# A four-stage decoder step: loading the SGU's output weights two tiles early, building two tables by doubling, and turning a constant later

## The chip, the cores and the metric

One NeuronCore of a Trainium2 chip runs the whole program. TensorE does the matrix products and transposes (through PSUM), VectorE, ScalarE and GpSimd the elementwise work, and SyncE issues nearly all DMAs. The metric is the device time of one execution in microseconds (us), the median of several runs. Lower is better.

## What is computed

One inference step of a decoder with two layers over 1024 prompt tokens and 8 sample tokens, all in float32. Layer 0 mixes tokens with a spatial gating unit (SGU), layer 1 with a sparse attention over the keys that an indexer picks. A gated convolutional MLP (ConvGLU) follows each. Every sub-layer is modulated by scales, shifts and gates from `c`, and is closed by a LayerNorm. Cut to what the change touches:

```python
def sgu_mixer(h, w_in, b_in, norm_g, norm_b, w_s, b_s, w_out):
    z = jax.nn.gelu(h @ w_in + b_in)
    u, v = jnp.split(z, 2, axis=-1)
    v = layer_norm(v, norm_g, norm_b)
    ...
    return (u * mixed) @ w_out, v          # w_out: 1024 x 1024, the "output pieces"

xp = post_norm(xp, yp, mp[:, 2], ln_g[i, 0], ln_b[i, 0])     # LayerNorm(ALPHA*x + (1+gate)*y)
fp, cp = conv_glu(modulate(xp, ...), ...)                    # a, u = h @ w_up; (gelu(conv(a)) * u) @ w_down

s_idx = sum over heads of relu(qi . ki) * wi                 # the indexer's scores
_, sel = lax.top_k(s_idx, n_keep)                            # 256 of 1024 keys, or 128 of 513 for a sample
```

## The kernel before

**Data and products.** The activations lie transposed, features on partitions and 1032 tokens along the free dimension, in three chunks `CH` of 384, 384 and 264 tokens. A float32 product is made of three fast ones: the weights are split into a high and a low half (`whi`, `wlo`), the activations too (`Hh`, `Hl`), and `mm3` (lines 86 to 89) adds hi x hi, hi x lo and lo x hi. `dense` (line 156) makes one 128-column weight piece times one chunk: 8 x 3 = 24 matmuls into a PSUM bank `psA`.

**Weights.** `load_w` (line 108) loads a piece of 512 KB with one DMA on SyncE into a `raw` buffer (three in all, shared with the loads of `ada_round` and some scratch), and `split` (line 99) makes the two halves. Its `eng` names the two engines: "GG" is GpSimd for both, "AV" ScalarE for the high and VectorE for the low half. The halves lie by default in the pool W (four buffers, so two pieces), or, if `pool` is given, in one of the tags T (13 buffers), P (2) and E (2).

**The order of instructions.** The text of the program is the order of priority. A planner that lays out the instructions when the program is built puts on each engine what is ready earliest by its own estimates, hands out the buffers of a tag in the order of the program, and sets the waits; on the chip each engine then runs its own list strictly in order.

**The end of the SGU.** The loop at line 605 makes the eight U tiles with pieces 8 to 15, while `pump` hands out steps from a queue `fq`: from i = 12 on the eight loads and products of `ada_round(0, 2)` and its end, in which VectorE adds at line 258. With the last piece (i = 15) the product of U and V is split into `Hh` (ScalarE) and `Hl` (VectorE, line 106), chunk by chunk. At the end of every turn `zload(i + 2)` (line 320) loads one piece: pieces 14 and 15 are the last of the input weights, and 16 to 23 are the eight output pieces, called 0 to 7 below (`dt` in the code). Pieces 0 and 1 go to W, the others to T; 2 to 7 are loaded behind the loop, at line 626.

**The output projection** (`out_proj`, line 640) runs over the three chunks and, in each, over the eight output pieces, so a piece is used three times and given back after its use in chunk 2. VectorE accumulates each result into R (`accumulate`, line 634). Behind a chunk `ln_steps` (line 406) is put into `fq`: `t1` normalises three blocks of 128 tokens (transposes into two `psB` banks, of four; statistics on VectorE, three small operations on GpSimd, two writes by ScalarE, line 400, into a tile `n`), and `t2` turns them back, eight times, and applies scale and shift (`apply`, line 365: ScalarE lines 371 and 379, VectorE 372, GpSimd's `Hl` 377). The first block's `n` of a chunk is an E tile, the second's a P tile, the third's a raw buffer. The first ConvGLU tile then takes E for `As` and P for `Cc` (line 699), and `wload` its weights.

**Constants of the sparse attention** (lines 795 to 831) are made between the ConvGLU of layer 0 and the indexer's projections: `bits` and `pows`, 31 powers of two as integers and as floats, one column at a time; `rmask`, a mask of 128 x 8, and its transpose `ET`, by one transpose on TensorE and one copy on VectorE. `bits` and `pows` are read by the searches for the k-th largest score (`search`, line 935), `ET` by the samples' attention (line 1321). `sample_scores` (line 1040) is the queue's part that scores the samples' keys.

Of the kernel before, what the change touches and what calls it, by code (L numbers as in the profile page):

```python
# [13 lines left out]
OP = mybir.AluOpType  # L14
# [6 lines left out]
T = NPT + NB  # L21
# [34 lines left out]
def hybrid_step(  # L56
# [7 lines left out]
    V, A, G, PE, SP = nc.vector, nc.scalar, nc.gpsimd, nc.tensor, nc.sync  # L64
# [12 lines left out]
    def Tt(name, dt=F32, tag="T", n=SLOT):  # L77
        return tp.tile([128, n], dt, name=name, tag=tag, bufs=BUFS[tag])

    def bank(tag="A"):  # L80
        return psum.tile([128, 512], F32, name="ps" + tag, tag="ps" + tag)
# [17 lines left out]
    def split(hi, lo, src, e_hi, e_lo):  # L99
        if e_hi == "A":  # L100
            A.activation(hi, src, AF.Copy)  # L101
        elif e_hi == "G":
            G.tensor_scalar(hi, src, 1.0, 0.0, op0=OP.mult, op1=OP.add)  # L103
        else:
            V.tensor_copy(hi, src)
        (V if e_lo == "V" else G).tensor_tensor(lo, src, f(hi), op=OP.subtract)  # L106

    def load_w(src, cols, pool=None, eng="GG"):

        n = KT * cols  # L110
        raw = raws.tile([128, SLOT], F32, name="raw", tag="raw")
        SP.dma_start(raw[:, :n].rearrange("p (k c) -> p k c", k=KT), src.rearrange("(k p) c -> p k c", p=128))
        if pool:
            hi, lo = Tt("whi", F32R, pool), Tt("wlo", F32R, pool)
        else:
            hi = wp.tile([128, SLOT], F32R, name="whi", tag="W")
            lo = wp.tile([128, SLOT], F32R, name="wlo", tag="W")
        split(hi[:, :n], lo[:, :n], raw[:, :n], eng[0], eng[1])
        return (hi[:, :n].rearrange("p (k c) -> p k c", k=KT), lo[:, :n].rearrange("p (k c) -> p k c", k=KT))
# [25 lines left out]
    fq = deque()  # L145

    def pump(n=1):
        for _ in range(n):
            if fq:
                fq.popleft()()  # L150

    def drain():
        while fq:
            fq.popleft()()

    def dense(w, cols, c, tag="A"):
        c0, n = CH[c]
        b = bank(tag)
        for k in range(KT):
            mm3(b[:cols, :n], (w[0][:, k, :cols], w[1][:, k, :cols]), (Hh[:, k, c0:c0 + n], Hl[:, k, c0:c0 + n]),  # L160
                k == 0, k == KT - 1)
        return b
# [21 lines left out]
    def tr(out, in_):  # L184
        PE.transpose(out, in_, ident[:in_.shape[0], :in_.shape[0]])  # L185
# [7 lines left out]
    b = bank("B")  # L193
# [124 lines left out]
    pieces = {}  # L318

    def zload(i):  # L320
        if i < 16:
            m = zorder[i]
            pieces[i] = load_w(win[:, m * 128:(m + 1) * 128], 128, eng="AV" if i < 2 else "GG")
        elif i < 24:
            dt = i - 16
            pieces[i] = load_w(sgu_w_out[0][:, dt * 128:(dt + 1) * 128], 128, pool=[None, None, "T", "T", "T", "T", "T", "T"][dt])


    def mod(L, i):
# [104 lines left out]
    b = bank("B")  # L434
# [103 lines left out]
    b = bank("B")  # L538
# [62 lines left out]
    def product(m, c):  # L601
        c0, n = CH[c]
        V.tensor_tensor(VT[m][:, c0:c0 + n], VT[m][:, c0:c0 + n], U[m][:, c0:c0 + n], op=OP.mult)

    for i in range(8, 16):
        m = i - 8
        U[m] = Tt("U", tag="PPTT"[m % 4])
        for c in range(3):
            b = dense(pieces[i], 128, c)
            c0, n = CH[c]  # L610
            A.activation(U[m][:, c0:c0 + n], b[:, :n], AF.Gelu_apprx_tanh, bias=PAR[:, pSBI + m:pSBI + 1 + m])
            pump(2 if i < 12 else 1)
            if i > 11:
                product(m, c)
            if i == 15:
                for k in range(8):
                    split(Hh[:, k, c0:c0 + n], Hl[:, k, c0:c0 + n], VT[k][:, c0:c0 + n], "A", "V")
        if i == 11:
            drain()
            for c in range(3):  # L620
                for k in range(4):
                    product(k, c)
            fq.extend(ada_round(0, 2, rawmk))
        zload(i + 2)
    drain()
    for i in range(18, 24):
        zload(i)
    gate = gates(0, 2, "g02")

# [168 lines left out]
    def carve(n, p=128):  # L798
        v = misc[:p, at[0]:at[0] + n]
        at[0] += n  # L800
        return v

    cmin, m01, bits, pows = carve(128), carve(256), carve(31).bitcast(I32), carve(31)
    onec, rmask, rep, ET, PN = carve(1), carve(8), carve(128, 8), carve(128, 8), carve(128, 8)
# [6 lines left out]
    V.memset(m01[:, 0:128], 0.0)  # L811
    V.tensor_scalar(m01[:, 128:256], cmin, 0.0, NEG, op0=OP.is_lt, op1=OP.mult)
    V.memset(onec, 1.0)
    for i in range(31):
        V.memset(bits[:, i:i + 1], 1 << i)
        V.memset(pows[:, i:i + 1], 0.5 * (1 << i))
    V.memset(rmask, 1.0)
    rv = rmask.rearrange("p (j e) -> p j e", e=2)
    G.affine_select(out=rv, in_=rv, pattern=[[-32, 4], [-8, 2]], compare_op=OP.is_ge, fill=0.0, base=0, channel_multiplier=1)
# [4 lines left out]
    for e in range(2):  # L824
        G.affine_select(out=rr[:, :, e, :], in_=rr[:, :, e, :], pattern=[[0, 4], [1, 8]], compare_op=OP.is_equal, fill=0.0, base=0,
                        channel_multiplier=-1)
    b = bank("B")
    tr(b[:8, 0:128], rmask)
    V.tensor_copy(ET, b[:8, 0:128])
    junk = Tt("junk", BF, n=2 * SLOT)  # L830
    junkV, junkA = junk[:, 0:1024], junk[:, 1024:2048]

# [207 lines left out]
    def sample_scores():  # L1040

        kc = [Tt("kc"), Tt("kc")]
        st = {}

        def load(h):
            for s in range(4 * h, 4 * h + 4):
                gather(kc[h][:, (s % 4) * 256:(s % 4 + 1) * 256], cki, s)

        def pair(ss):
            if not st:  # L1050
                st["p"] = bank("A")
            kt = Tt("kt", tag="E")
            for i, s in enumerate(ss):
                b = bank("B")
                for r in range(4):
                    o = (s % 4) * 256 + r * 64
                    tr(b[0:64, r * 128:(r + 1) * 128], kc[s // 4][:, o:o + 64])
                A.activation(kt[0:64, i * 512:(i + 1) * 512].rearrange("d (p r) -> d r p", r=4),
                             b[0:64, :].rearrange("d (r p) -> d r p", r=4), AF.Copy)
            for i, s in enumerate(ss):  # L1060
                r0, e = 32 * (s // 2), s % 2
                PE.matmul(st["p"][r0:r0 + 32, :512], QSI[:, s, :], kt[0:64, i * 512:(i + 1) * 512], start=(e == 0), stop=(e == 1),
                          skip_group_check=True)
        def end():
            SS = Spk[3][0][:, 512:1026]
            rl = rawmk()
            A.activation(rl[:, :512], st["p"], AF.Relu, scale=0.125)
            pn = bank("B")
            for s in range(NB):
                r0, e = 32 * (s // 2), s % 2  # L1070
                PE.matmul(pn[r0:r0 + 32, :8], QSI[:, s, :], kiT, start=(e == 0), stop=(e == 1), skip_group_check=True)
            A.activation(rl[:, 512:520], pn[:, :8], AF.Relu, scale=0.125)
            b = bank("B")
            mm(b[:, :8], rep, wisT, True, True)
            V.tensor_tensor(WM, b[:, :8], rmask, op=OP.mult)
            b, b2 = bank("B"), bank("B")
            mm(b[:8, :512], WM, rl[:, :512], True, True)
            mm(b2[:8, :8], WM, rl[:, 512:520], True, True)
            V.tensor_copy(SS[:8, :512], b[:8, :512])
            V.tensor_tensor(t88, b2[:8, :8], ident[0:8, 0:8], op=OP.mult)  # L1080
            V.tensor_reduce(SS[:8, 512:513], t88, axis=AX.X, op=OP.add)
            V.memset(SS[:8, 513:514], 0.0)
            starts("s")

        return [lambda: load(0), lambda: load(1)] + [lambda x=x: pair(x) for x in ((0, 2), (1, 3), (4, 6), (5, 7))] + [end]
# [4 lines left out]
    def starts(key):  # L1090
        ready.add(key)
        for name, eng, keys in PLAN:
            if key in keys and ready.issuperset(keys):
                items = [(k, S(k), 128, 128 * (k + 1), KEEP_P) if k != "s" else (k, Spk[3][0][:8, 512:512 + NS], 8, NS, KEEP_S)
                         for k in keys]
                sq[eng].append(search(name, items, eng))
# [3 lines left out]
    for c in range(3):  # L1100
        while c not in spilled:
            pump()
        ki_part(c)
        pump(PUMP[c])
        for t in range(4):
            qi_part(t, c)
            if (t, c) == (0, 2):
                dload(5)
                dload(6)
            pump(PUMP[c])  # L1110
            spin(*SPIN[0])
        fq.append(lambda c=c: ki_rows(c))
        for b in blocks_of(c):
            if 2 <= b < 8:
                fq.extend(idx_steps(b))
                fq.append(lambda b=b: starts(b))
    fq.extend(sample_scores())


# [31 lines left out]
    for w in range(2):  # L1151
        kf = [Tt("kf0", tag="P"), Tt("kf1", tag="P")]
        for kvh in range(2):
            i = 5 + 2 * w + kvh
# [3 lines left out]
            for c in range(3):  # L1158
                b = dense(pcs[i], 128, c)
                c0, n = CH[c]  # L1160
# [334 lines left out]
```

## Time and profile before

| | us |
|---|---|
| median of 3 runs (lowest to highest) | 2628.93 (2626.52 to 2629.45) |
| the profiled execution | 2626.55 |
| its span, first to last instruction | 2624.8 |
| TensorE busy in it | 2525.8 (96%) |
| VectorE / GpSimd / ScalarE busy | 1676.1 / 998.4 / 793.2 |
| its mean granted TensorE clock | 0.981 of full |

The span starts at 0, and all times below are from there. The SGU's input products run to about 290 us, its output projection to about 398, the first ConvGLU to about 1215, the sparse attention to about 1800 and the second ConvGLU to the end. A row of a timeline gives the start, the duration, the engine, the line, the operation, what it writes and reads and the count; in brackets stands how long the engine was idle before it, and what it waited for last by the profile. Such a releaser is inferred: where the engine named had long been done, it was another, often a DMA. Operations of one engine can overlap in the rows, since they are pipelined.

### The profile page before, as it was taken

What the parts mean: (1) busy time and instruction counts of PE and PEld (TensorE: products, weight loads), DVE (VectorE), ACT (ScalarE), POOL (GpSimd) and SP (SyncE); (2) the same over time, 40 slices, a digit from 0 to 9 for tenths busy, and PEclk for the clock granted to TensorE, in tenths of its full rate; (3) what the DMA queues carried; (4) which work ended last, traced back from release to release, by engine and by line L of the source; (5) the groups of instructions that cost most, each with busy time, mean ns of one, the idle gap of its engine ahead of it and who ended that gap; (6) DMA issues with size and microseconds to landing.
All of it is one profiled execution on the core that took longest, in us unless ns stands there. A gap on an engine that the chain in (4) does not pass through costs nothing.

```text
span 2624.8 us, 41121 instructions
## 1 busy us (share of the span) xinstructions
PE 2525.8 (96%) x15984; PEld 2369.4 (90%) x15984; DVE 1676.1 (64%) x3913; ACT 793.2 (30%) x1611; POOL 998.4 (38%) x1066
## 2 busy tenths in 40 slices
PE   7999999999999999999999989998999999999996
PEld 5898898999999999998887979777999999999996
DVE  4233346677677767755798987534767677767647
ACT  3121234111111111124576776542311111111121
POOL 3332535233222322335346665534523333222335
PEclk8999999999999999999999989999999999999998
DMA  8314302222222222111114112233211111111111
GB/s 274 124 51 127 105 17 71 91 81 73 89 81 81 89 66 96 60 34 51 60 39 118 42 47 65 69 121 109 65 49 49 49 49 41 41 49 49 49 41 67
DMA packets 203977, 192.15 MB, mean 73 GB/s; under 512 B 9806, under 2 KB 178246, under 8 KB 202999
## 3 DMA queue, kind: packets, MB, share of 16 engines
q1 hardware_dynamic: 200582, 179.86, 21.8%
q0 software_dynamic: 2688, 9.44, 1.1%
q8 instruction: 127, 2.08, 0.3%
q14 instruction: 67, 0.55, 0.1%
q10 hardware_dynamic: 513, 0.23, 0.0%
HBM read 178.41 MB, written 11.27 MB: 72 GB/s over the span
## 4 chain that ended last, share of the span: by engine, by line
PE 80%; DVE 11%; POOL 3%; issue 2%; ACT 2%; DMA 2%; ACTq 0%; SPq 0%; POOLq 0%; DVEq 0%
PE psA L84 50%; PE psB L84 23%; PE psB L185 3%; PE psB L245 2%; DVE Cc L714 2%; DVE junk L948 1%; DVE R L634 1%; PE psA L185 1%; ACT junk L979 1%; DVE S L928 1%; POOL L L1252 0%; DMA raw<-in_dsa_w_out_dram 0%; DMA adaw<-in_w_ada_dram 0%; DVE R L638 0%; PE psA L1308 0%
## 5 line engine op out<-in xcount | busy, mean ns | idle before, releaser
L84 PE MATMUL psA<-Hh,whi 128*128 128x384 f32 (+1 forms) x2896 | 935.6, 324 | 14.7 <-POOL whi L103 7.7
L84 PE MATMUL psA<-Hl,whi 128*128 128x384 f32 (+1 forms) x2896 | 932.4, 322 | 0.1
L84 PE MATMUL psA<-Hh,wlo 128*128 128x384 f32 (+1 forms) x2896 | 929.1, 321 | 0.9 <-DVE wlo L106 0.9
L634 DVE SCALAR_TENSOR_TENSOR R<-psB,g,R 128x384 f32<-128x384 f32 (+1 forms) x952 | 525.6, 568 | 296.0 <-PE psB L84 293.8
L103 POOL TENSOR_SCALAR whi<-raw 128x1024 fp32r<-128x1024 f32 x179 | 194.8, 1089 | 1100.7 <-PE psA L84 962.2
L84 PEld LDWEIGHTS psA<-Hh,whi 128*128 128x128 f32 x2896 | 548.0, 189 | 44.8 <-issue 21.5
L84 PEld LDWEIGHTS psA<-Hl,whi 128*128 128x128 f32 x2896 | 548.6, 189 | 7.2 <-issue 6.1
L84 PEld LDWEIGHTS psA<-Hh,wlo 128*128 128x128 f32 x2896 | 547.9, 189 | 7.6 <-issue 5.0
L106 POOL TENSOR_TENSOR wlo<-raw,whi 128x1024 fp32r<-128x1024 f32 x163 | 403.6, 2476 | 12.7
L84 PE MATMUL psB<-gh,whi 128*128 128x384 f32 (+1 forms) x1056 | 341.9, 324 | 3.4 <-DVE t L637 1.6
L84 PE MATMUL psB<-gl,whi 128*128 128x384 f32 (+1 forms) x1056 | 337.7, 320 | 0.0
L84 PE MATMUL psB<-gh,wlo 128*128 128x384 f32 (+1 forms) x1056 | 337.7, 320 | 0.0
L714 DVE SCALAR_TENSOR_TENSOR Cc<-As,PAR,Cc 128x256 f32<-128x256 f32 (+3 forms) x264 | 262.2, 993 | 56.1 <-ACT Cc L709 54.9
L84 PEld LDWEIGHTS psB<-gh,whi 128*128 128x128 f32 x1056 | 198.4, 188 | 25.6 <-issue 13.8
L84 PEld LDWEIGHTS psB<-gl,whi 128*128 128x128 f32 x1056 | 198.6, 188 | 0.0
L84 PEld LDWEIGHTS psB<-gh,wlo 128*128 128x128 f32 x1056 | 198.5, 188 | 0.0
L101 ACT ACTIVATE gh<-Cc 128x384 fp32r<-128x384 f32 x132 | 64.9, 492 | 437.7 <-DVE Cc L721 437.6
L716 ACT ACTIVATE Cc<-Cc 128x384 f32<-128x384 f32 x132 | 64.9, 492 | 391.2 <-DVE Cc L714 391.2
L708 ACT ACTIVATE As<-psA 128x384 f32<-128x384 f32 x132 | 60.5, 458 | 341.5 <-PE psA L84 341.5
L721 DVE TENSOR_TENSOR Cc<-psA,Cc 128x384 f32<-128x384 f32 x132 | 67.8, 513 | 111.9 <-PE psA L84 111.3
L84 PE MATMUL psB<-Hh,wh 128*128 128x384 f32 (+1 forms) x512 | 137.8, 339 | 1.0 <-POOL wh L103 0.5
L638 DVE TENSOR_TENSOR R<-R,t 128x8 f32<-128x8 f32 x328 | 131.0, 406 | 2.9
(362 smaller groups left out, 3299.6 us busy)
## 6 DMA issues: line engine op xcount, KB each, us to landing
raw<-in_ffn_w_up_dram SPq DMA_DIRECT2D x88, 512.0 KB
raw<-in_w_ada_dram SPq DMA_DIRECT2D x64, 512.0 KB
raw<-in_ffn_w_down_dram SPq DMA_DIRECT2D x44, 512.0 KB
adaw<-in_w_ada_dram SPq DMA_DIRECT2D x32, 512.0 KB
raw<-in_sgu_w_in_dram SPq DMA_DIRECT2D x16, 512.0 KB
raw<-in_dsa_w_in_dram SPq DMA_DIRECT2D x16, 512.0 KB
raw<-in_dsa_w_out_dram SPq DMA_DIRECT2D x32, 256.0 KB
raw<-in_sgu_w_out_dram SPq DMA_DIRECT2D x8, 512.0 KB
```

What stands on the lines that cost most here:

```text
L84: PE.matmul(out, l, r, start=start, stop=stop)
L101: A.activation(hi, src, AF.Copy)
L103: G.tensor_scalar(hi, src, 1.0, 0.0, op0=OP.mult, op1=OP.add)
L106: (V if e_lo == "V" else G).tensor_tensor(lo, src, f(hi), op=OP.subtract)
L185: PE.transpose(out, in_, ident[:in_.shape[0], :in_.shape[0]])
L245: PE.matmul(st["b"][32 * g:32 * g + 32, :512], SCT[:, k, :], rw[g // 2][:, (g % 2) * 512:(g % 2 + 1) * 512], start=(k == 0), stop=(k == KT ...
L634: V.scalar_tensor_tensor(R[c][:, dt, :npr], b[:, :npr], gp[:, dt:dt + 1], R[c][:, dt, :npr], op0=OP.mult, op1=OP.add)
L638: V.tensor_tensor(R[c][:, dt, npr:n], R[c][:, dt, npr:n], t8, op=OP.add)
L708: A.activation(As[:, c0:c0 + n], b[:, :n], AF.Copy)
L714: V.scalar_tensor_tensor(Cc[:, a0:c0 + npr], As[:, a0 - d:c0 + npr - d], w, Cc[:, a0:c0 + npr], op0=OP.mult, op1=OP.add)
L716: A.activation(Cc[:, c0:c0 + n], Cc[:, c0:c0 + n], AF.Gelu_apprx_tanh)
L721: V.tensor_tensor(Cc[:, c0:c0 + n], b[:, :n], Cc[:, c0:c0 + n], op=OP.mult)
```

## The change

The load of the output pieces is moved up and spread. At the end of the turn i = 14 pieces 1, 0 and 2 are loaded, in this order, and at i = 15 none; 3 to 7 follow behind the loop. Piece 1 goes from W to T, piece 2 from T to both buffers of E, piece 3 from T to W. Pieces 3, 5 and 7 are split by ScalarE and VectorE, the others by GpSimd as before. The table `pows` is made by one fill and five multiplications that double its length, and `bits` by one multiplication that converts it, in place of 62 fills. The transpose of `rmask` and its copy into `ET` become a step of the queue just ahead of the samples' scores.

```diff
@@ zload
-            pieces[i] = load_w(sgu_w_out[0][:, dt * 128:(dt + 1) * 128], 128, pool=[None, None, "T", "T", "T", "T", "T", "T"][dt])
+            pieces[i] = load_w(sgu_w_out[0][:, dt * 128:(dt + 1) * 128], 128, pool=[None, "T", "E", None, "T", "T", "T", "T"][dt],
+                               eng="AV" if dt in (3, 5, 7) else "GG")
@@ the loop over i = 8 .. 15
-        zload(i + 2)
+        if i < 14:
+            zload(i + 2)
+        elif i == 14:
+            for n in (17, 16, 18):
+                zload(n)
     drain()
-    for i in range(18, 24):
+    for i in range(19, 24):
         zload(i)
@@ constants
-    for i in range(31):
-        V.memset(bits[:, i:i + 1], 1 << i)
-        V.memset(pows[:, i:i + 1], 0.5 * (1 << i))
+    V.memset(pows[:, 0:1], 0.5)
+    for n in (1, 2, 4, 8, 16):
+        m = min(n, 31 - n)
+        V.tensor_scalar(pows[:, n:n + m], pows[:, 0:m], float(1 << n), None, op0=OP.mult)
+    V.tensor_scalar(bits, pows, 2.0, None, op0=OP.mult)
...
-    b = bank("B")
-    tr(b[:8, 0:128], rmask)
-    V.tensor_copy(ET, b[:8, 0:128])
@@ behind the indexer's projections
+    def turn_rmask():
+        b = bank("B")
+        tr(b[:8, 0:128], rmask)
+        V.tensor_copy(ET, b[:8, 0:128])
+
+    fq.append(turn_rmask)
     fq.extend(sample_scores())
```

## Rows read from the trace of the kernel before

**Rows 1.** The page's first part: busy us, share of the span, instructions.

```profile
PE 2525.8 (96%) x15984; PEld 2369.4 (90%) x15984; DVE 1676.1 (64%) x3913; ACT 793.2 (30%) x1611; POOL 998.4 (38%) x1066
```

**Rows 2.** Timeline of TensorE, 276 to 316 us: start, duration, [idle, releaser].

```profile
290.01 0.35 PE L84 MATMUL psA<-Hh,whi 128*128 128x384 f32 x1
...
294.05 0.33 PE L84 MATMUL psA<-Hh,wlo 128*128 128x384 f32 x1
299.57 0.69 PE L84 MATMUL psA<-Hh,whi 128*128 128x384 f32 x1 [5.19 <-POOL whi L103]
...
303.88 0.34 PE L84 MATMUL psA<-Hh,wlo 128*128 128x384 f32 x1
```

**Rows 3.** Windows: PE, PEld, DVE, ACT, POOL busy (count), PEclk, DMA, GB/s.

```profile
300.00:302.00 2.00, 2.00 (x8) 2.00 (x8) 0.00 (x0) 0.00 (x0) 2.00 (x2) 0.50 0.06 18
```

**Rows 4.** Timeline of SyncE's DMA issues, 274 to 303 us.

```profile
275.01 0.38 SPq L112 DMA_DIRECT2D raw<-in_sgu_w_out_dram  x1
...
278.25 0.38 SPq L112 DMA_DIRECT2D raw<-in_sgu_w_out_dram  x1
...
283.29 0.99 SPq L112 DMA_DIRECT2D raw<-in_sgu_w_out_dram  x2
...
297.35 0.37 SPq L112 DMA_DIRECT2D raw<-in_sgu_w_out_dram  x1
```

**Rows 5.** Timeline of GpSimd, 225 to 345 us.

```profile
279.70 2.65 POOL L106 TENSOR_TENSOR wlo<-raw,whi 128x1024 fp32r<-128x1024 f32 x1
287.00 1.72 POOL L103 TENSOR_SCALAR whi<-raw 128x1024 fp32r<-128x1024 f32 x1 [4.65 <-DVE Bs L358]
288.80 8.51 POOL L106 TENSOR_TENSOR wlo<-raw,whi 128x1024 fp32r<-128x1024 f32 x1
297.29 2.23 POOL L103 TENSOR_SCALAR whi<-raw 128x1024 fp32r<-128x1024 f32 x2
```

**Rows 6.** Timeline of VectorE, 225 to 345 us.

```profile
285.03 0.49 DVE L258 TENSOR_TENSOR MOD<-psB,PAR 128x36 f32<-128x36 f32 x4
...
287.70 1.04 DVE L356 TENSOR_TENSOR Bp<-Bp,MOD 128x8 f32<-128x8 f32 x1
...
295.61 2.00 DVE L106 TENSOR_TENSOR Hl<-V,Hh 128x264 fp32r<-128x264 f32 x1 [0.49 <-ACT Hh L101]
```

**Rows 7.** Lines 106 and 101 by form: duration min/median/max in ns.

```profile
L106 POOL TENSOR_TENSOR wlo<-raw,whi x163: 1427/2400/8514, 75.9 to 2539.5; 128x1024 fp32r<-128x1024 f32 x162, 128x576 fp32r<-128x576 f32 x1
L106 DVE TENSOR_TENSOR wlo<-raw,whi x18: 1206/1225/1372, 35.5 to 1822.4; 128x1024 fp32r<-128x1024 f32 x18
L101 ACT ACTIVATE whi<-raw x2: 1049/1050/1051, 31.9 to 36.2; 128x1024 fp32r<-128x1024 f32 x2
```

**Rows 8.** Timelines of VectorE, ScalarE and GpSimd, then a window, 330 to 440 us.

```profile
380.64 0.48 DVE L634 SCALAR_TENSOR_TENSOR R<-psA,g,R 128x256 f32<-128x256 f32 x1 [2.15 <-PE psA L84]
398.39 0.48 DVE L634 SCALAR_TENSOR_TENSOR R<-psA,g,R 128x256 f32<-128x256 f32 x1 [2.14 <-PE psA L84]
352.49 2.36 ACT L371 ACTIVATE Hh<-psB,Bp,Gp 128x384 fp32r<-128x384 f32 x4 [2.95 <-PE psB L185]
360.96 3.94 POOL L377 TENSOR_TENSOR Hl<-ht,Hh 128x384 fp32r<-128x384 f32 x4 [3.04 <-DVE ht L372]
405.43 1.02 POOL L377 TENSOR_TENSOR Hl<-ht,Hh 128x384 fp32r<-128x384 f32 x1 [2.82 <-DVE ht L372]
434.16 0.76 POOL L377 TENSOR_TENSOR Hl<-ht,Hh 128x264 fp32r<-128x264 f32 x1 [0.17 <-DVE ba L362]
420.00:440.00 20.00, 16.62 (x99) 13.82 (x100) 19.11 (x46) 8.68 (x19) 14.20 (x13) 1.00 0.21 63
```

**Rows 9.** Line 816 and line 829, and TensorE's timeline, 1190 to 1300 us.

```profile
L816 DVE MEMSET misc<- x31: 59/59/59, 1215.4 to 1220.0; 128x1 f32 x31
L829 DVE COPY misc<-psB x1: 259/259/259, 1223.5 to 1223.5; 8x128 f32<-8x128 f32 x1
1220.91 1.97 PE L185 MATMUL psA<-ident,R 128*128 128x128 f32 x8 [2.66 <-ACT n L400]
```

## The prediction, made before the change was run

> **What bounds the kernel now.** I read the page's busy shares first: TensorE is busy for 96% of the span [rows 1]. So a microsecond off another engine counts only where TensorE stands still for it, and each edit is priced from the stretch it sits in. For the first edit I read TensorE's timeline around the end of the SGU. The 24 matmuls of output piece 0 on chunk 0 start between 290.01 and 294.05 us, 0.176 us apart; then TensorE is idle for 5.19 us, released by a high half (whi) that GpSimd wrote, and the next 13 starts, from 299.57 to 303.88, take 4.31 us where 13 x 0.176 = 2.28 would do [rows 2]. The granted clock there is 0.50, the lower level of 1.2 GHz [rows 3]. The hole is worth 5.2 + 2.0 = 7.2 us.
>
> Next, why the piece was late: SyncE's, GpSimd's and VectorE's timelines of the same stretch. Output pieces 0 and 1 are loaded at 275.01 and 278.25 us, pieces 2 and 3 at 283.29, and piece 4 at 297.35 [rows 4]. Piece 1 is in memory by about 281.8 (a load takes 278.57 - 275.01 = 3.56 us, where GpSimd's first split begins 1.13 us ahead of the row at 279.70). But it lies in the weight pair W, whose buffers the last U piece uses until 290. GpSimd went on to piece 2 at 287.00, and the low half of piece 2 took 8.51 us [rows 5] where the median of 163 such is 2.40 [rows 7]. VectorE was working back to back beside it, and its first gap was the 0.49 us before 295.61 [rows 6]. Only then did piece 1's high half come, at 297.29, in a pair of 2.23 us [rows 5]. So the hole has two causes: the buffer of piece 1, and GpSimd kept out by VectorE.
>
> **The change part by part. Loads and splits.** Piece 1 now has T buffers and is loaded first, then piece 0, then piece 2 (in both E buffers). The three loads still pass through the three raw buffers that the ada_round's weights and its scratch tile leave one by one. Hence I keep their times, 275.01, 278.25 and 283.29 [rows 4], with other names: the lines stand earlier in the program, but SyncE can't issue earlier. Each issue is one DMA, as before, and nothing else is queued on SyncE ahead of them. Piece 1 is split from 278.57 to 282.35. Piece 0 is there at 281.8 and must be split by 290.0. GpSimd meets VectorE's Hl subtractions; they end in the four L258 additions at 285.03, which read PSUM [rows 6], so I let GpSimd in there: 1.05 + 2.4 us from 285.1 gives 288.6, or 290 with one more wait. That is in time. Piece 2 is loaded by 286.9 and must be split by 290.0 + 2 x 24 x 0.176 = 298.4. VectorE's stream, which broke at 295.1, is now longer by the 3.45 us that piece 0's split takes from it, and breaks at 298.6; a low half after that ends at 301. If GpSimd slips into an earlier gap, as the split at 287.00 did between two dependent additions (the one at 287.70 then took 1.04 us [rows 6]), piece 2 is in time. The hole that is left lies between 0 and 2.6 us, or 4.6 with the lower clock. I take 2 us at the full clock, nearer to the upper row because the stream was unbroken in the trace. **The gain is 7.2 - 2 = 5.2 us.**
>
> The pieces on ScalarE and VectorE (3, 5, 7) cost 1.05 us and 1.22 us each [rows 7]. Piece 3 waits for W until 290. Behind it on ScalarE are the last Hh copies and on VectorE the last Hl subtractions, both for chunks 1 and 2, which TensorE reads 34 us later. It is needed at 302.6, so it costs nothing, or 1.2 us if its low half goes ahead of piece 2's. Pieces 4 to 7 follow at 4.2 us apiece, more than the 3.5 us that GpSimd needs for one; with half of them on other engines none is late.
>
> **The E pair, a wait that the change adds.** Piece 2 now holds both E buffers until its last use, chunk 2 of the output projection: in the trace that accumulation is at 380.64 [rows 8]. The first normalised block of each chunk (t1 of blocks 0, 3, 6) needs an E buffer, and so does the first ConvGLU tile As. In the trace chunk 0's transposed apply ran from 352.49 to 360.96 + 3.94 = 364.90 [rows 8], beside the matmuls of chunk 1. Now block 0's ScalarE write waits to 381, with two of the four psB banks in its hand. Behind it nothing can pass: chunk 0's transposes, then chunk 1's. In the time frame of the trace (take 5.2 off for the real one), chunk 0 is done at 381 + 12.4 = 393.5; TensorE wants it after the output projection, whose last accumulation is at 398.39 [rows 8], so there it costs nothing. Chunk 1 was done at 405.43 + 1.02 = 406.5 and chunk 2 at 434.16 + 0.76 = 434.9 [rows 8], a distance of 28.5 us, in which TensorE had its own pauses: 3.4 us of the 20 from 420 on [rows 8]. What counts is when chunk 2 ends now, since the matmuls after it follow without a gap. If each chunk trails the one before by 12.4 us (the pace of an apply that nothing disturbs) the end is at 418, and TensorE, with 16.8 us of other matmuls to do, would even save up to the 3.4 us of pauses; by 28.5 us it is 450.5, a loss of 15.6. I take 21.5, near the middle, since the statistics of one chunk can run beside the apply of another but GpSimd also splits ConvGLU weights then: 393.5 + 43 = 436.5, **a loss of about 2 us** (-3.4 to +15.6). W's second pair now comes free with piece 3, 7 us later than with piece 1; its next user is the up half of the first ConvGLU tile, wanted at 398 + 4.2 = 402: nothing.
>
> **Tables by doubling.** 62 fills of 59 ns [rows 9] are 3.7 us of VectorE's busy time, but they overlap each other and share 4.6 us with other work. Seven operations of which each doubling needs the last come in their place; at 0.26 us (the small copy of [rows 9]) they would be 1.8 us. TensorE waits in that stretch, 2.66 us before 1220.91 [rows 9], for a normalised block whose statistics stand between the fills. Bounds: 2.7 gained, 1.8 lost. I take 0, because the block's statistics, and not the fills, fill VectorE there.
>
> **The constant turned later.** One transpose and one 0.26 us copy [rows 9] leave a stretch in which TensorE is behind and enter the sample's scores, with a psB bank. Bounds +0.3 and -0.3; taken 0. Its reader, the sample's attention, comes later in the program.
>
> **The sum.** -5.2 + 2 + 0 + 0 = -3.2 us. The profiled execution took 2626.55 us (span 2624.8 and 1.75 around it), which gives 2623.35; the median of the three runs is 2628.93, 2.38 above the profiled one, so **2625.7 us**.
>
> **A rule that speaks against the change.** In the trace GpSimd's low half took 8.51 us while VectorE subtracted SBUF tiles from each other, and the 264-column subtraction after it took 2.00 us [rows 5, 6]. The Trainium skill, SBUF — State Buffer, section "SBUF: two separate sides", says the two engines share a port pair that is locked for a whole instruction when VectorE has two SBUF inputs, and that the loser waits. By that rule, with which the two rows agree, the low halves on VectorE are not a second path beside GpSimd's: this is the third rival.
>
> **The rivals.** (1) *Both waits vanish.* Piece 2 is split in an early gap and the normalisations fit under the output projection's tail and the first ConvGLU matmuls: -7.2, at best with a microsecond or two of TensorE's pauses at 420 as well. For it: TensorE has 16.8 us of matmuls between chunk 0 and chunk 2. Against it: the 8.51 us row. 2621.7 us (2619 to 2623.5). (2) *The E pair decides.* The chunks trail each other by the 28.5 us that chunk 2 took in the trace: +15.6 - 5.2 = +10.4, 2639 us. It makes the kernel slower when chunk 2's end moves by more than the 5.2 us gained, that is from a distance of 23 us, and by over 0.2% from 26 us. For it: two psB banks are held and GpSimd has splits to do; against it: 28.5 us held waits on loads and on ConvGLU work that don't double. (3) *The change doesn't do what it says:* the raw buffers give the loads the same times, VectorE keeps GpSimd out of piece 0 or 2 for another 6 us as it did between 288.80 and 295.1, and the hole only moves: 0 + 2, 2631 us.
>
> **How the numbers follow.** About 0.2%, 5.3 us, is what a measurement of this kernel can tell from no change. The forecast (within it) has 0.45, rival 1 (faster) 0.35, rival 2 (slower) 0.15, rival 3 (within) 0.05. So faster 0.35, same 0.50, slower 0.15. The range goes from rival 1's lower part, 2619, to 2634, where rival 2's milder half is still in; its far end and a little on the other side stay out.
>
> **What would show it.** Right: two W or T pieces split before 290 and no idle over 3 us on TensorE from 290 to 310, full clock there; ScalarE's first normalised block of layer 0 at about 375 (380.6 less the gain), beside chunk 2's matmuls and not chunk 1's; pauses on TensorE between the output projection and the second ConvGLU tile of 4 to 7 us in place of 3.4. Wrong: an idle of 5 us before 310 (rival 3); chunk 2's last Hl subtraction over 5 us later against the end of the output projection than now (rival 2); that subtraction no later (rival 1); or a gain or loss after 500 us, which none of this explains and which a new order of instructions from the planner would have made.

## The result and the profile after

| | us |
|---|---|
| median of 4 runs after (lowest to highest) | 2644.62 (2640.86 to 2647.51) |
| median of 4 runs before beside them | 2627.72 (2621.88 to 2629.45) |
| ratio, with its 95% interval | 1.0067 (1.0047 to 1.0088) |
| the profiled execution after, and its span | 2647.51, 2645.7 |

The change makes the kernel slower by 16.9 us, 0.67%. Forecast was 2625.7 with a range of 2619 to 2634, so the time lies outside the range, on the side of rival 2 and 5.6 us beyond its 2639.

The first part of the page of the changed kernel: TensorE is busy 9.2 us longer than in [rows 1] with as many instructions. So of the 20.9 us by which the span grew, nearly half is slower matmuls (the mean granted clock of this execution is 0.978, that of the profile before 0.981) and the rest is pauses. The profile shows the slowest of the four executions after.

```profile
PE 2535.0 (96%) x15984; PEld 2375.1 (90%) x15984; DVE 1685.0 (64%) x3861; ACT 798.2 (30%) x1614; POOL 985.4 (37%) x1060
```

**The hole is nearly closed.** TensorE's timeline around the end of the SGU, and the window of [rows 3], changed kernel:

```profile
298.01 0.44 PE L84 MATMUL psA<-Hl,whi 128*128 128x384 f32 x1 [1.87 <-DVE Hl L106]
...
300.00:302.00 2.00, 2.00 (x14) 2.00 (x13) 2.00 (x6) 0.77 (x2) 0.00 (x0) 1.00 0.00 0
```

An idle of 1.87 us at the full clock stands where [rows 2, 3] have 5.19 us and then half clock. But the releaser is another: TensorE waits for Hl, the low half of the activations, and not for a weight. VectorE's and GpSimd's timelines of the changed kernel say why:

```profile
280.91 11.72 DVE L106 TENSOR_TENSOR Hl<-V,Hh 128x384 fp32r<-128x384 f32 x7 [1.31 <-ACT Hh L101]
293.87 2.37 DVE L348 TENSOR_SCALAR Gp<-MOD 128x8 f32<-128x8 f32 x1
...
281.11 2.63 POOL L106 TENSOR_TENSOR wlo<-raw,whi 128x1024 fp32r<-128x1024 f32 x1
285.15 2.61 POOL L106 TENSOR_TENSOR wlo<-raw,whi 128x1024 fp32r<-128x1024 f32 x1
289.64 2.58 POOL L106 TENSOR_TENSOR wlo<-raw,whi 128x1024 fp32r<-128x1024 f32 x1
293.63 2.58 POOL L106 TENSOR_TENSOR wlo<-raw,whi 128x1024 fp32r<-128x1024 f32 x1
```

Four low halves run on GpSimd at their usual 2.6 us. Three of them fall beside VectorE's seven subtractions, which take 11.72 us, and the fourth beside a small operation (L348) that takes 2.37 us where its twin in the kernel before took 0.17. In the kernel before, with one low half beside them, the same seven took 5.59, in its VectorE timeline:

```profile
279.52 5.59 DVE L106 TENSOR_TENSOR Hl<-V,Hh 128x384 fp32r<-128x384 f32 x7 [1.31 <-ACT Hh L101]
```

**The wait for the E pair is new.** The view of ScalarE's waits from 340 to 450 us (waited in total, times, longest), then ScalarE's first normalised block, GpSimd's Hl subtractions of the three chunks with the ConvGLU weights between them, and the last accumulation of the output projection, all of the changed kernel:

```profile
ACT n L401 <- PE psA L84: 26.0, 1, 26.0
...
372.41 1.45 ACT L401 ACTIVATE n<-psB,mv 128x512 f32<-128x512 f32 x2 [26.00 <-PE psA L84]
...
383.34 3.92 POOL L378 TENSOR_TENSOR Hl<-ht,Hh 128x384 fp32r<-128x384 f32 x4 [1.52 <-DVE ht L373]
397.95 1.96 POOL L378 TENSOR_TENSOR Hl<-ht,Hh 128x384 fp32r<-128x384 f32 x2 [1.90 <-DVE ht L373]
399.88 2.37 POOL L106 TENSOR_TENSOR wlo<-raw,whi 128x1024 fp32r<-128x1024 f32 x1
...
411.14 2.44 POOL L106 TENSOR_TENSOR wlo<-raw,whi 128x1024 fp32r<-128x1024 f32 x1
...
414.90 1.02 POOL L378 TENSOR_TENSOR Hl<-ht,Hh 128x384 fp32r<-128x384 f32 x1
...
437.96 0.75 POOL L378 TENSOR_TENSOR Hl<-ht,Hh 128x264 fp32r<-128x264 f32 x1 [1.43 <-DVE ba L363]
...
391.51 0.48 DVE L639 SCALAR_TENSOR_TENSOR R<-psA,g,R 128x256 f32<-128x256 f32 x1 [0.66 <-PE psA L84]
```

Chunk 0 is done at 383.34 + 3.92 = 387.3, chunk 1 at 415.9 and chunk 2 at 438.7. From the end of the output projection to the end of chunk 2 it is now 438.7 - 392.0 = 46.7 us; in [rows 8] it was 434.9 - 398.9 = 36.0. TensorE's pauses in that stretch of the changed kernel, and the windows behind them:

```profile
392.99 0.44 PE L185 MATMUL psB<-ident,n 128*128 128x128 f32 x2 [0.62 <-ACT n L401]
...
395.91 0.44 PE L185 MATMUL psB<-ident,raw 128*128 128x128 f32 x2 [1.81 <-ACT raw L401]
...
425.24 0.38 PE L185 MATMUL psB<-ident,raw 8*128 8x8 f32 x2 [3.51 <-ACT raw L401]
428.38 0.78 PE L84 MATMUL psA<-Hh,whi 128*128 128x264 f32 x2 [1.13 <-DVE Hh L377]
...
420.00:430.00 10.00, 5.36 (x30) 3.75 (x28) 5.87 (x18) 6.70 (x14) 2.74 (x5) 0.70 0.00 0
430.00:440.00 10.00, 10.00 (x60) 9.10 (x60) 7.54 (x26) 4.98 (x10) 5.64 (x8) 0.79 0.16 55
```

From 420 to 440 TensorE is busy for 15.4 us at a clock of 0.70 to 0.79, where [rows 8] have 16.6 at 1.00: the pauses are paid twice.

**A loss after 1200 us.** For this table each instruction outside TensorE was matched with the same one of the kernel before, and the median shift of its start was taken in each stretch; a column is how much the shift grew there (us, plus is later). One profile each, so read single numbers of 1 to 3 us with care, and the last column not as the price of an edit: in that stretch three kernels with the constant at its old place lose 3.3 to 3.5 us too, and the one profile of the change without the E pair, with the constant moved, loses 0.5. The last section tells what happens there.

| kernel | up to 500 | 1180 to 1300 | 1300 to 1750 | 1750 to 1865 | 1865 to 1930 |
|---|---|---|---|---|---|
| the change | +6.7 | +2.2 | +3.0 | +4.5 | +4.3 |
| first edit alone | +10.5 | +0.5 | -2.8 | +0.9 | +0.1 |
| constant alone | +2.1 | +1.5 | +0.6 | +0.8 | +4.3 |
| tables alone (two runs) | +1.5, +0.1 | +2.1, +1.1 | +0.3, -0.1 | -2.5, -1.4 | -0.2, -0.1 |

### The profile page after: what moved, and what is told of

The parts are those of the page before. It is cut to its first block, busy times and chain, and to the rows that moved or that the text cites. A ratio compares the mean times of both kernels' runs of the same rounds, so it can differ in the third digit from the quotient of the medians.

```text
span 2645.7 us, 41035 instructions
## 1 busy us (share of the span) xinstructions
PE 2535.0 (96%) x15984; PEld 2375.1 (90%) x15984; DVE 1685.0 (64%) x3861; ACT 798.2 (30%) x1614; POOL 985.4 (37%) x1060
## 4 chain that ended last, share of the span: by engine, by line
PE 78%; DVE 12%; POOL 3%; DMA 3%; ACT 3%; issue 2%; ACTq 0%; SPq 0%; DVEq 0%; POOLq 0%
PE psA L84 49%; PE psB L84 22%; PE psB L185 3%; PE psB L245 2%; DVE Cc L719 1%; DVE junk L952 1%; PE psA L185 1%; DVE S L932 1%; ACT junk L983 1%; DVE R L639 1%; DMA raw<-in_dsa_w_out_dram 1%; DVE wh L106 1%; DVE Hl L106 0%; DVE L L1257 0%; ACT Hh L372 0%
## 5 line engine op out<-in xcount | busy, mean ns | idle before, releaser
L106 POOL TENSOR_TENSOR wlo<-raw,whi 128x1024 fp32r<-128x1024 f32 x160 | 391.6, 2447 | 12.4
```

## The experiments

Each ratio is to the kernel before, run beside it on the same chip; 0.001 is 2.6 us, and an interval is about 0.0015 to either side, so a difference of two ratios is known to about 0.002, or 5 us. The first four undo or isolate a part each.

**The first edit alone,** tables and constant as before.

```diff
+pool=[None, "T", "E", None, "T", "T", "T", "T"][dt],
+eng="AV" if dt in (3, 5, 7) else "GG"
...
+            for n in (17, 16, 18):
+                zload(n)
```

> Only the first edit (loads, buffers and engines of the SGU's output pieces); tables and the turned constant as in the kernel before. Theory: the E pair costs about 11 us between the output projection and the second ConvGLU tile, the hole at 294 us gives back about 6, and the attention stage keeps its old order, so 5 to 6 us slower than before, some 2633, with the attention's own length as before. Rival: the attention's extra 13 us come from layer 0's new timing; then this kernel is already 17 us slower, 2644.

Measured 1.0028 (1.0013 to 1.0043), 7.4 us slower. That is near the theory's 5 to 6 us and far from the rival's 17. Its waits repeat the change's: ScalarE's n waits 26.0 us for psA, TensorE pauses 3.3 us for raw at 427 us. At the hole it has the same pause as the change, but with the lower clock behind it:

```profile
296.72 0.44 PE L84 MATMUL psA<-Hl,whi 128*128 128x384 f32 x1 [1.87 <-DVE Hl L106]
...
298.00:300.00 2.00, 2.00 (x8) 2.00 (x7) 2.00 (x6) 0.06 (x1) 0.00 (x0) 0.50 0.00 0
```

The first edit is a loss by itself, and it is not the whole of the 1.0067.

**The first edit without the E pair.**

```diff
-pool=[None, "T", "E", None, "T", "T", "T", "T"][dt]
+pool=[None, "T", "T", None, "T", "T", "T", "T"][dt]
```

> The first edit alone, with piece 2 in T buffers as before in place of E. Theory: without the E pair the wait of the normalised blocks is gone and the 6 us of the hole remain: 2621 to 2622, the first normalised block of chunk 0 beside the matmuls of chunk 1 again. Rival (the loss in layer 0 comes from the splits on ScalarE and VectorE or from the later W pair, not from E): 5 us slower than before, 2633.

Measured 0.9998 (0.9983 to 1.0013). Against the first edit alone this is 0.0030 less: the E pair costs about 8 us. But the gain that I expected once the wait is gone isn't there, and the rival's loss of 5 us neither. TensorE's and VectorE's timelines of this kernel show that the hole is still half open:

```profile
299.60 0.63 PE L84 MATMUL psA<-Hh,whi 128*128 128x384 f32 x2 [2.58 <-ACT Hh L101]
301.81 0.69 PE L84 MATMUL psA<-Hl,whi 128*128 128x384 f32 x1 [0.20 <-DVE Hl L106]
...
280.04 11.86 DVE L106 TENSOR_TENSOR Hl<-V,Hh 128x384 fp32r<-128x384 f32 x7 [1.31 <-ACT Hh L101]
```

TensorE again waits for activations, behind subtractions that took 11.86 us beside GpSimd's low halves. By 340 us TensorE has gained 2.7 us in this profile, and keeps them to 420; by 440 us 0.2 is left, behind a pause with a lower clock that the last section shows.

**The constant alone, and the tables alone,** first the one diff, then the other:

```diff
-    tr(b[:8, 0:128], rmask)
-    V.tensor_copy(ET, b[:8, 0:128])
...
+    fq.append(turn_rmask)
```

```diff
-    for i in range(31):
-        V.memset(bits[:, i:i + 1], 1 << i)
-        V.memset(pows[:, i:i + 1], 0.5 * (1 << i))
+    V.memset(pows[:, 0:1], 0.5)
+    for n in (1, 2, 4, 8, 16):
...
```

> Only the third edit, the transpose of rmask and its copy moved into the queue ahead of the samples' scores. Theory (the planner orders the attention stage anew, and the new order costs): 8 to 13 us slower than before, 2636 to 2641, all of it after 1215 us. Rival (the move is one transpose and a copy): within 1 us of before.

Measured 1.0025 (1.0010 to 1.0040): 6.6 us for one transpose and one 0.26 us copy that only moved, less than the theory's 8 to 13 and well beyond the rival's 1.

> Only the second edit, the tables by doubling. Theory (planner's new order): a difference of up to 10 us either way, after 1215 us, with no difference before. Rival (only VectorE's own instructions count): within 2 us of before.

Measured 1.0014 (1.0000 to 1.0028). The three parts are 0.0028, 0.0025 and 0.0014 above 1, together 0.0067, the whole; that it fits so well is luck, with about 0.0015 on each. So neither the tables nor the constant look free, though neither adds work worth the name. What they change is the order: set side by side with the trace of the kernel before, 498 of TensorE's 15984 matmuls and transposes stand elsewhere with the tables alone, 593 with the constant alone, from about 1200 us on through the attention. With the first edit alone only 49 do there, and the rest of its changes lie in the SGU's output and the normalisation behind it. (The expectations below count 856, 251 and 155 rows of 15304; the traces give 498, 157 and 79 of 15984.)

**GpSimd out of the way.** In the first edit without E, all eight pieces on ScalarE and VectorE:

```diff
-eng="AV" if dt in (3, 5, 7) else "GG"
+eng="AV"
```

> The first edit alone, with two changes: output piece 2 in T and not in E, and all eight output pieces split by ScalarE (high) and VectorE (low), none by GpSimd. What is asked is what still delays chunk 0 at 298 us. Theory A (two engines on one port): in the run without E the seven subtractions of Hl from 280 us took 11.9 us beside GpSimd's low halves of 2.6 us, and TensorE then stood still for 2.6 us and ran at the lower clock. With no low half on GpSimd the seven take about 5.6 us again (as in the kernel before), three low halves on VectorE add 3 x 1.22 = 3.7 us, and the stream ends 2.6 us sooner: no idle over 1 us and the full clock from 290 to 310, a shift of -6 to -7 us at 340 us against the kernel before (-2.8 in the run without E), and 2.3 of it lost again at 420 where the clock falls: about -4 us in the end. Theory B (VectorE's own amount of work): the seven subtractions stay long or the three low halves move them back as far, TensorE stands still for 2.5 us or more, the shift at 340 us is -3 or less, and the time is within 2 us of the kernel before.

Measured 0.9981 (0.9969 to 0.9992), **faster than both kernels**. VectorE's timeline and the windows from 280 to 310 us of this kernel (its PE, PEld, DVE, ACT, POOL busy, then the clock):

```profile
281.68 2.66 DVE L106 TENSOR_TENSOR Hl<-V,Hh 128x384 fp32r<-128x384 f32 x5 [1.31 <-ACT Hh L101]
...
280.00:290.00 10.00, 10.00 (x61) 9.67 (x60) 8.30 (x20) 8.96 (x16) 0.00 (x0) 1.00 0.55 156
290.00:300.00 10.00, 10.00 (x65) 10.00 (x64) 10.00 (x25) 8.54 (x19) 0.00 (x0) 1.00 0.47 129
300.00:310.00 10.00, 10.00 (x59) 10.00 (x58) 6.70 (x10) 2.12 (x2) 0.00 (x0) 1.00 0.48 138
```

GpSimd does nothing here, a subtraction takes 2.66 / 5 = 0.53 us in place of 11.86 / 7 = 1.69, TensorE never stops and keeps the full clock. From 285 to 340 us the shift of TensorE's own matmuls goes from +2.2 to -5.2: 7.4 us gained, what the hole was worth (7.2). Theory A holds.

**The constant turned twice.** Both the old place and the new one:

```diff
     tr(b[:8, 0:128], rmask)
     V.tensor_copy(ET, b[:8, 0:128])
...
+    fq.append(turn_rmask)
     fq.extend(sample_scores())
```

> The kernel before with the constant turned twice: at its old place and once more ahead of the sample's scores. One transpose and one 0.26 us copy more than before, none missing. The order of the instructions is then unchanged up to about 1370 us, and changed after it on TensorE (251 rows of 15304) and VectorE (382 of 3808). Theory A (the new order costs the time, not the operation): the turned constant alone cost +2.6 to +10.5 us, of which its profile showed +2 between 1250 and 1300 us and the rest behind 1700; this kernel keeps the first part as it was and changes only a part of the rest: 0 to +6 us, with the shift at 1300 us at 0. Theory B (the transpose and copy in the sample's scores cost it): the same +2.6 to +10.5 as the turned constant alone, and the loss starts where they stand, with VectorE's copy or a psB bank as what TensorE waits for. Theory C (taking them out of the old place costs it): 0, within 2 us.

Measured 0.9990 (0.9979 to 1.0002). The operation in its new place costs nothing, so theory B falls. By the numbers A and C both stand. What is left as the cause is that it is gone from the old place, and with it the old order from 1210 to 1370 us, which this kernel keeps; the order behind 1370 us is another than with the constant alone, so the two aren't told apart.

**Fills and doublings.** The 62 fills stay, the seven operations come behind them:

```diff
         V.memset(pows[:, i:i + 1], 0.5 * (1 << i))
+    V.memset(pows[:, 0:1], 0.5)
+    for n in (1, 2, 4, 8, 16):
+        m = min(n, 31 - n)
+        V.tensor_scalar(pows[:, n:n + m], pows[:, 0:m], float(1 << n), None, op0=OP.mult)
+    V.tensor_scalar(bits, pows, 2.0, None, op0=OP.mult)
```

> The kernel before with its 62 fills kept and the seven doublings written after them on top (the same values): all the work of both. The order of the other instructions is then changed only from about 1210 to 1300 us (155 rows on TensorE), where the tables alone changed 856 rows up to 1900 us. Theory A (the new order in the attention stage cost the 0 to +7 us of the tables alone): 0, within 2 us, although VectorE has 3.7 us of fills more than with the tables alone. Theory B (the chain of seven dependent operations costs it, beside the block's statistics): +2 to +7, with more idle on TensorE between 1210 and 1250 us than the 4.6 us of the kernel before.

Measured 0.9994 (0.9983 to 1.0005). All the work of both tables is free, and less of it, in the tables alone, seems not to be (1.0014). TensorE's pauses at the tables, first of this kernel, then of the tables alone in their second run:

```profile
1218.91 0.66 PE L185 MATMUL psA<-ident,R 128*128 128x128 f32 x4 [1.31 <-ACT R L379]
1222.22 1.97 PE L185 MATMUL psA<-ident,R 128*128 128x128 f32 x8 [2.66 <-ACT n L400]
```

```profile
1229.68 0.44 PE L185 MATMUL psA<-ident,raw 128*128 128x128 f32 x2 [1.49 <-ACT raw L400]
1233.16 0.69 PE L185 MATMUL psA<-ident,n 128*128 128x128 f32 x2 [1.91 <-ACT R L379]
1236.03 0.69 PE L185 MATMUL psA<-ident,n 128*128 128x128 f32 x2 [1.33 <-ACT R L379]
```

The first pair is that of the kernel before [rows 9]. In the second TensorE turns the normalised blocks back (reads of raw and n) without other matmuls between them, and waits for ScalarE each time. The same three waits are in both runs of the tables alone, and four like them in every kernel with the moved constant, the first three of them here as in the changed kernel:

```profile
1237.46 0.69 PE L185 MATMUL psA<-ident,raw 128*128 128x128 f32 x2 [4.07 <-ACT raw L401]
1240.95 0.69 PE L185 MATMUL psA<-ident,n 128*128 128x128 f32 x2 [0.88 <-ACT R L380]
1243.18 0.69 PE L185 MATMUL psA<-ident,n 128*128 128x128 f32 x2 [0.69 <-ACT R L380]
```

**Doublings, then fills; and the tables alone again.** The same operations as the last kernel in the other sequence, which gives the order of the tables alone:

```diff
+    V.memset(pows[:, 0:1], 0.5)
+    for n in (1, 2, 4, 8, 16):
...
     for i in range(31):
         V.memset(bits[:, i:i + 1], 1 << i)
         V.memset(pows[:, i:i + 1], 0.5 * (1 << i))
```

> The same operations as the kernel with fills and doublings (62 fills and the seven doublings), written the other way round: the doublings first, the fills behind them. Only their sequence in the program differs, but now the order of the other instructions is that of the tables alone (856 rows of TensorE's 15304 changed against the kernel before, up to about 1900 us), where fills first changed 155 rows and gave a ratio of 0.9994. Theory A (the order that comes out for the attention stage costs the time of the tables alone, 1.0014): 1.001 to 1.003, +3 to +7 us, with VectorE's operations on the tables no longer than in the other kernel. Theory B (the order costs nothing, the 1.0014 of the tables alone was chance or lay in the operations): 0.999 to 1.001.

> The tables by doubling alone, a second time and in more rounds, beside the kernel with the same order and the fills on top. The first time it gave 1.0014 (1.0000 to 1.0028). Theory A (the order costs it): again 1.001 to 1.003 and within 0.001 of the kernel with doublings and then fills. Theory B (chance, or the operations): within 0.001 of the kernel before.

Measured 1.0005 (0.9994 to 1.0016) and 1.0014 (1.0002 to 1.0026). The price of the tables came out a second time, with an interval that just clears 1; that the order alone makes it is not shown: 1.0005 lies in theory B's range, and its interval reaches into theory A's. The pauses of the tables alone are there in the profile, in the kernel of doublings and then fills too (1.49, 1.92 and 1.33 us). From 1180 to 1300 us the shift grew by 3.0 in it. Over all profiles, the seven with these pauses grew by 1.1 to 3.0 us in that stretch (mean 1.9), the six that keep the pauses of [rows 9] by -1.0 to +0.6 (mean 0.0). So **1.9 us of the loss after 1200 us is located**; the rest of what the two edits cost is told below.

**The change without the E pair,** then **the change mended** (without E and with all pieces on ScalarE and VectorE), both as a diff to the changed kernel:

```diff
-pool=[None, "T", "E", None, "T", "T", "T", "T"][dt],
+pool=[None, "T", "T", None, "T", "T", "T", "T"][dt],
...
-eng="AV" if dt in (3, 5, 7) else "GG"
+eng="AV"
```

The first has the pool alone.

> The whole change with one thing undone: output piece 2 in a T pair and not in the E pair. The wait of the normalisations for the E pair is taken away, the rest of the change stays. Theory A (the three parts add up: 1.0028 for the first edit, 1.0025 and 1.0014 for the other two make the 1.0067 of the whole, and without E the first edit gave 0.9998): 1.0037, that is +9.7 us, in place of +17.5, with ScalarE's first normalised block of layer 0 beside chunk 1 of the output projection again and no idle over 2 us between 380 and 440 us. Theory B (the E pair is the whole of the loss, and the other parts only look like one): within 0.1% of the kernel before. Theory C (the E pair's wait is made up for by later pauses): 1.006 or more, as the whole change.

Measured 1.0029 (1.0018 to 1.0041): nearest to theory A's 1.0037, which its interval holds, and clear of B and C. It is 0.0038 less than the whole change, so the E pair costs 10 us here against 8 alone. The longest wait of ScalarE's n in the same view is now for statistics, 13.9 us, and none is for psA:

```profile
ACT n L401 <- POOL mv L390: 16.2, 3, 13.9
```

> The whole change with its first edit mended: output piece 2 in T, all eight pieces split by ScalarE and VectorE; the tables and the turned constant as in the changed kernel. Theory A (each part keeps its price when the others are there): the mended first edit gave 0.9980 and the other two cost 1.0031 (1.0029 of the change without E against 0.9998 of the first edit without E), together 1.0011: +1 to +5 us, with no idle on TensorE between 285 and 310 us and the loss behind 1200 us. Theory B (the tables and the constant cost only beside a late first stage): 0.998 to 0.999, as the mended first edit alone.

Measured 0.9998 (0.9987 to 1.0010), a miss for both theories by a hair: between them. TensorE has no idle from 280 to 310 us here, and gains the same 7.4 us at the hole. The other two edits cost 0.9998 / 0.9980 = 1.0018 here, 1.0031 beside the first edit without E, and 1.0039 as the sum of the two alone: 5 to 10 us, each known to about 5 us.

**The faster version again,** the kernel of the first 0.9981:

> The version that was faster than both, a second time: the first edit with output piece 2 in T and all eight pieces split by ScalarE and VectorE. The first time it gave 0.9981 (0.9969 to 0.9992). If the hole at 298 us is what it gains (about 7 us there, shown in its first profile), the ratio is again 0.997 to 0.999, with no idle on TensorE between 285 and 310 us; if the first time was chance, it is within 0.001 of 1.

Measured 0.9980 (0.9965 to 0.9995), no idle and a clock of 1.00 from 280 to 310 us once more, and again 7.4 us gained there. It is faster by 5 us, 0.2%.

## Why the prediction was wrong, point by point

- **The hole, "-7.2 + 2": the size is right, the path is not.** 1.87 us at the full clock are left where I put 2, and TensorE gains 5.2 us there, the very number. That is luck: the first edit alone has the same pause with the lower clock behind it and gains 3.7. And I had VectorE keep GpSimd out, as the 8.51 us row did; here GpSimd, with four pairs to split back to back, kept VectorE out (11.72 us for seven subtractions against 5.59). I took VectorE's subtractions for a stream that nothing disturbs and never asked what the earlier splits do to them. The runs with no GpSimd there show the cause: 7.4 us gained in each of three profiles. By the Trainium skill, SBUF — State Buffer, section "SBUF: two separate sides", the ports that VectorE and GpSimd share are an exclusive lock: when VectorE's operation has two SBUF inputs and GpSimd's reads SBUF, whichever starts first has them for its whole instruction and the other waits. The rows of both kernels agree, one for each way round: in the changed kernel one subtraction begins within 0.4 us of the start of each of the three low halves and ends 0.4 us behind it (2.7 to 2.8 us in place of 0.55), and in the kernel before the low half of 8.51 us ends 2.2 us after VectorE's stream breaks.
- **The E pair, "a loss of about 2 us": this term failed.** The place was right (the block waits to 372.4, I had about 375; nothing behind it passes), the pace was not. I took 21.5 us from chunk to chunk; it was 28.7 and 22.8, or 25.7 a chunk. In that time GpSimd spent 10.4 us on ConvGLU weights between the Hl subtractions (399.88, 411.14 above) and ScalarE waited 7.5 us for statistics; that these set the pace is my reading, and no run isolates it. By the prediction's own working, 51.4 us for two chunks in place of 43 is 8.4 more, 10.4 in all, and the runs say 8 and 10. I had argued that the 28.5 us of [rows 8] would not double. The first distance repeated it, the second came near my 21.5, and the mean lies nearer to the trace's own row than to the middle between it and a bound that nothing in the trace reached.
- **The lower clock behind the pauses** (0.70 and 0.79) was not in the E term at all. I had priced it for the hole and left it out here.
- **Tables, "0", and constant, "0": failed, beyond both bounds.** 3.7 and 6.6 us alone (the bounds were 1.8 and 0.3), 5 to 10 together. The bounds held for the operations (turned twice 0.9990, fills and doublings 0.9994) and not for the edit. The planner put other instructions elsewhere, which the prediction named among what would make it wrong, after 500 us, and gave no chance and no width. 1.9 us are shown at the normalisation at 1220 to 1245 us. About one more microsecond is seen where the sample's block is normalised in the attention's output, at about 1860 us: all four profiles with the moved constant, and none of the others, have TensorE wait 0.6 to 0.9 us for it, and the pause behind it takes 1.40 us in place of 1.18. In all four the granted clock then falls, to 0.50 to 0.72 over 5 us, and the shift grows by about 2 to 6 us from 1850 to 1890; of the ten others four show a fall there and six none. So a part of the rest may lie here, but that is too few profiles to say. Where the rest goes, 2 to 7 us, stays open, and that it is the order was argued from these waits and not shown: doublings and then fills, with the order of the tables alone, gave 1.0005.
- **The rivals.** Rival 2 came out by its own sign: chunk 2's last subtraction 46.7 us behind the output projection in place of 36.0, over 5 later. Its 2639 is 5.6 us short, about what the other two edits cost. Rival 3, the hole that only moves, is what the first edit without E became (2.58 us of idle, 0.9998), by VectorE and not by GpSimd.
- **The chances.** 0.15 on slower was rival 2 alone. With the trace's 28.5 as the likelier pace, and a width of 5 us or more on edits that reorder a planned program, slower would have been the forecast; both are said with the result known.

## What to carry to other kernels

Before a tile is put into a buffer pair that a later stage needs, take that stage's pace from its own rows as it is, not halfway to an ideal, and add the clock that TensorE loses in the new pauses. When work is moved earlier onto GpSimd, list what VectorE has to deliver in that window: here each of the two engines in turn kept the other waiting. Where a planner orders the program, price even a null edit by re-ordering, and compare the order of the instructions before trusting a sum of durations.

## What the runs showed of the hardware that was not expected

**The same pause costs the clock in one execution and not in another.** A pause of 1.17 us on TensorE, in the normalisation at 420 us, stands in the kernel before and in the first edit without E. First the rows of the kernel before, then those of the other (pause; window with the clock):

```profile
421.02 0.48 PE L84 MATMUL psA<-Hh,whi 128*128 128x264 f32 x2 [1.17 <-DVE Hh L376]
...
422.00:426.00 4.00, 4.00 (x29) 3.43 (x28) 3.88 (x15) 3.16 (x7) 2.30 (x3) 1.00 0.01 2
```

```profile
418.92 0.47 PE L84 MATMUL psA<-Hh,whi 128*128 128x264 f32 x2 [1.17 <-DVE Hh L377]
...
422.00:426.00 4.00, 4.00 (x17) 3.48 (x17) 2.77 (x9) 2.04 (x4) 2.54 (x4) 0.50 0.00 0
```

A clock of 0.50, the lower level of 1.2 GHz, and 17 matmuls in place of 29 in the same 4 us: 2.5 us of the 2.7 gained at the hole are gone by 440 us. This isn't the edit: the kernels with only the constant or the tables changed run the instructions of the kernel before up to 1200 us. Behind the same 1.17 us pause the clock fell, to 0.59 to 0.66 over 5 us, in the profiles of the constant alone, of fills and doublings, and of doublings then fills, which lost 2.1 to 2.4 us each by 460 us; it stayed at 1.00 in those of the tables alone (both runs) and of the constant turned twice. The twin pause in the second ConvGLU does it again, 1.18 us at 1857.29 in the kernel before and 1.17 at 1858.83 in the other; the window of the same 10 us, in the same order:

```profile
1860.00:1870.00 10.00, 10.00 (x71) 9.63 (x71) 9.62 (x24) 4.83 (x11) 7.73 (x8) 1.00 0.15 54
```

```profile
1860.00:1870.00 10.00, 10.00 (x51) 9.08 (x51) 7.05 (x26) 5.19 (x10) 5.92 (x8) 0.66 0.17 55
```

Here the shift grew by 3.4 us. What decides was not found; the profiles of one and the same kernel differ in it (from 1840 to 1930 us the version with GpSimd out of the way lost 6.0 us in its first profile and nothing in its second). The profile of the kernel before has the full clock behind both pauses, so a shift against it counts such a fall as a loss. So a gain of 2 or 3 us that moves such a pause can't be read from one profile.

**GpSimd's splits and VectorE's subtractions** hold each other up: 0.53 us for a subtraction alone, 1.69 beside low halves, and 8.51 for a low half beside subtractions [rows 5]. Seven subtractions alone would be 3.7 us; with the three low halves beside them, 7.8 us together, that makes 11.5 of the 11.72 measured, as if the two took turns.
